# Nine step times in the planner of a state-space and attention trunk

## The chip, the cores and the metric

The kernel runs on one core of a Trainium2 chip. The metric is device microseconds (us) of one execution. Engines are called by their short names: PE is TensorE (matrix products; PEld is its weight load), DVE is VectorE, ACT is ScalarE, POOL is GpSimd, SP is the engine whose queue issues nearly all DMAs.

## The reference, cut to what matters

One call computes a trunk of two layers for 1024 latent tokens and 256 context tokens of width 1024: a state-space mixer (layer 0), attention (layer 1) and a final norm. The change touches the first layer alone:

```
z, xbc, dt = split(h @ in_w)                    # 2048 z, 4096 xbc, 64 dt columns
xbc = silu(conv of 5 taps along the tokens (xbc))
xs, B, C = split(xbc)                           # 8 groups of 4 heads of 64; B and C of 128 per group
la  = cumsum over 128 tokens of dt * a          # forward and backward in time
states = B^T (exp(la_end - la) * dt * xs)       # per chunk of 128 tokens
prev   = running sum of the states, decayed by exp(la_end)
y  = (C B^T * exp(la_l - la_s) * dt, causal) xs + (C prev) * exp(la)
out = rmsnorm((y_forward + y_backward + d * xs) * silu(z)) @ out_w
```

All of it is float32. A product of two float32 matrices is made from three matmuls on the parts "high" and "low" of each operand (`mm3`, L168 to L170).

## The kernel before, in words

The first layer, but for its output projection, is a list of steps and not a program written in order; two more such lists follow it, for the output projection and for the second layer. Each step is made by `plan.op(engine, function, after, rank, us, takes, uses)`: the engine that runs it, the steps it must follow, a rank (lower is sooner) and `us`, the time that the planner believes it takes. `takes` and `uses` name buffers from rings of fixed size. `Plan.order()` then plays all the steps through once, before the kernel is built: at each moment every engine that is free starts, of its steps whose inputs are ended and whose buffers are free, the one of lowest rank. The order in which steps were started there is the order in which their instructions are emitted. On the chip each engine works through its own queue strictly in that order, and waits where an input isn't there. So the numbers `us` change no instruction; they change which instruction stands ahead of which.

The steps around the change, for one core and all 1280 tokens (ten chunks of 128, in blocks of 256, 512 and 512):

- **Projections** (`load`, `project`): 48 tiles of 128 columns, 32 for the convolution and 16 for z. A tile's weights come in two halves `wraw`; ACT copies the high part `whi` (L599), and POOL and DVE in turn make the low part `wlo` (L602). PE makes 24 triples `pj` (L168 to L170).
- **Convolution** (`conv_tile`): ACT evicts the products to `ub` (L636) and makes the first tap (L642), DVE adds four taps (L645), ACT applies silu (L650). A ring of six tiles `ch` holds the results.
- **Mixing** (`mix`), once for each of eight groups, after its four convolution tiles: PE transposes (`tc`, L690), DVE or ACT copies to `xst` (L697, L695) and ACT to `Bt` (L701). `state`: POOL scales `xw` (L713), PE makes `st` (L718, two per step, nine steps), POOL decays the last state into `tm` (L732), DVE adds both into `PV` (L736). `wmat`: SP brings `lab` (L750), POOL masks it (L754), ACT takes four exponentials into `W` (L760), DVE adds the two directions (L773) and multiplies by the product of B and C (L775, with PE's L770), PE makes `yd` (L795). `y_out`: SP brings `es` (L832), PE makes `yo` (L837), DVE weighs it into `es` (L841), POOL or DVE adds up (L854), SP stores `y_d` (L861).
- **Columns for later** (`mod_later`): DVE accumulates rows of a weight for the second layer into `macc` (L900, L902), adds a bias (L923) and makes a low part (L931).
- Before all that: PE sums the columns of the first modulation (L304), the inputs are normalised and transposed (L331 to L367), and the step sizes `dv` are projected (L439 to L442, L453).

The planner fills PE with projections of later tiles and of z wherever a step of the mixing isn't ready.

Of the kernel before, what the change touches and what calls it, by code (L numbers as in the profile page):

```python
# [39 lines left out]
URGENT, LATE, DT_RANK = 30., 40., 15.  # L40
# [105 lines left out]
def emit(tc, A, out):  # L146
    nc = tc.nc
    V, S, G, T, Q = nc.vector, nc.scalar, nc.gpsimd, nc.tensor, nc.sync
# [106 lines left out]
    for b in ub:  # L255
# [4 lines left out]
    plan = Plan({"piece": 20, "xt": 4, "raw": 4, "wraw": 2, "mraw": 2, "wparts": 4, "pj": 2, "ub": 2, "ch": NCH, "zs": 2, "tc": 2,  # L260
                 "st": 1, "yd": 1, "yo": 1, "xst": 1, "Bt": 1, "PV": 1, "xw": 3, "tm": 1, "lab": NLAB, "W0": 2, "W1": 2, "es": 3})
# [321 lines left out]
    te_op, u_op, la_op, e_op, dec_ops = decays(step_sizes())  # L583
# [3 lines left out]
    def load(src, after=(), rank=0., raws="wraw"):  # L587

        raw, parts, t = plan.hold(raws), plan.hold("wparts"), {}
        odd = plan.turn("wlo")  # L590

        def bring():
            t["w"] = WR.raw_tile()
            Q.dma_start(t["w"], src)

        def high():
            t["hi"] = BIG.tile([128, 512], FR, tag="whi", bufs=4, name="whi")
            t["lo"] = BIG.tile([128, 512], FR, tag="wlo", bufs=4, name="wlo")
            S.activation(t["hi"], t["w"], AF.Copy)  # L599

        def low():
            (G if odd else V).tensor_tensor(t["lo"], t["w"], t["hi"].bitcast(FT), op=OP.subtract)  # L602

        a = plan.op("SP", bring, after, rank - 40, takes=[raw])
        a = plan.op("ACT", high, [a], rank - 30, .627, takes=[parts], uses=[raw])
        a = plan.op(*(("POOL", low, [a], rank - 30, 1.44) if odd else ("DVE", low, [a], rank - 30, .80)),
                    uses=[raw, parts])
        return t, parts, a

# [19 lines left out]
    def conv_tile(ct, rank):  # L629

        u, out, t = plan.hold("ub"), plan.hold("ch"), {}
        i, evs = plan.count("ub"), []
        for lo, hi, pt, bank, mm in project(16 + ct, rank):
            def evict(lo=lo, hi=hi, pt=pt):
                o = 2 if lo == 0 else 4
                S.activation(ub[i % 2][:, lo + o:hi + o], pt["p"], AF.Copy)  # L636
            evs.append(plan.op("ACT", evict, [mm] + evs[:1], rank - 1e4, .585 if hi - lo > 256 else .375,
                               takes=[u] if lo == 0 else [], uses=[u, bank]))

        def first():  # L640
            t["a"] = CH.tile([128, CW], FT, tag="ch", name="acc")
            S.activation(t["a"], ub[i % 2][:, 0:CW], AF.Copy, scale=convw[:, ct, 0:1])  # L642

        def tap(k):
            V.scalar_tensor_tensor(t["a"], ub[i % 2][:, k:k + CW], convw[:, ct, k:k + 1], t["a"], op0=OP.mult, op1=OP.add)  # L645

        a = plan.op("ACT", first, evs + [rest[0]], rank - URGENT, 1.364, takes=[out], uses=[u])
        for k in range(1, 5):
            a = plan.op("DVE", lambda k=k: tap(k), [a], rank - URGENT, 1.70, uses=[u, out])
        a = plan.op("ACT", lambda: S.activation(t["a"], t["a"], AF.Silu, bias=convb[:, ct:ct + 1]), [a, rest[1]], rank - URGENT, 1.367,  # L650
                    uses=[out], table="silu")
        return t, out, a
# [12 lines left out]
    def mix(g, chs, rank):  # L665
# [6 lines left out]
        def op(eng, f, after, us, **kw):  # L672
            seq[0] += .01
            return plan.op(eng, f, after, rank + seq[0], us, **kw)

        s = {}
        hxst, hBt, hPV = plan.hold("xst"), plan.hold("Bt"), plan.hold("PV")
        ready, blocks = {}, {}
# [27 lines left out]
        def state(i):  # L706
            bank, t, mms = plan.hold("st"), {}, []
            for d, c in ((0, i), (1, BORD[i])):
                hw = plan.hold("xw")

                def scale(d=d, c=c):
                    t[d] = pool["now"].tile([128, 4, 64], FT, tag="xw", bufs=3, name="xw")
                    G.tensor_tensor(t[d], s["xst"][:, c], te_t[:, d, c, h4][:, :, None].to_broadcast([128, 4, 64]), op=OP.mult)  # L713

                def product(d=d, c=c):
                    if d == 0:
                        t["st"] = psum("st", [128, 2, 4, 64])
                    T.matmul(flat(t["st"][:, d]), s["Bt"][:, c, :], flat(t[d]), start=True, stop=True)  # L718

                a = op("POOL", scale, [ready[c][0], te_op], .80, takes=[hw], uses=[hxst])  # L720
                mms.append(op("PE", product, [a, ready[c][1]] + mms, .44, takes=[bank] if d == 0 else [], uses=[bank, hw, hBt]))
            if i == 0:
                def keep():
                    s["PV"] = pool["now"].tile([128, 9, 2, 4, 64], FT, tag="PV", name="PV")
                    S.activation(s["PV"][:, 0], t["st"], AF.Copy)
                pv[0] = op("ACT", keep, mms, .604, takes=[hPV], uses=[bank, hPV])
            else:
                ht = plan.hold("tm")

                def decay():  # L730
                    t["tm"] = pool["now"].tile([128, 2, 4, 64], FT, tag="tm", bufs=1, name="tm")
                    G.tensor_tensor(t["tm"], s["PV"][:, i - 1], dec_t[:, i, :, h4][:, :, :, None].to_broadcast([128, 2, 4, 64]),  # L732
                                    op=OP.mult)

                a = op("POOL", decay, [pv[0]] + dec_ops, 1.11, takes=[ht], uses=[hPV])
                pv[0] = op("DVE", lambda: V.tensor_tensor(s["PV"][:, i], t["tm"], t["st"], op=OP.add), [a] + mms, .68,  # L736
                           uses=[ht, hPV, bank])

        def wmat(c):

            t0, t, ws, bank = tok0(c), {}, [], plan.hold("tc")
            for d in range(2):
                hl, hw = plan.hold("lab"), plan.hold(f"W{d}")
                sgn = 1 - 2 * d

                def bring(d=d):
                    t["l", d] = pool["now"].tile([128, 4, 128], FT, tag="lab", bufs=NLAB, name="lab")
                    src = bass.AP(tensor=la_d.tensor, offset=la_d.offset + (c * 64 + d * 32 + g * 4) * 128,
                                  ap=[[0, 128], [1, 512]])
                    Q.dma_start(flat(t["l", d]), src)  # L750


                def close(d=d, sgn=sgn):
                    G.affine_select(t["l", d], t["l", d], [[0, 4], [sgn, 128]], OP.is_ge, NEVER, base=0,  # L754
                                    channel_multiplier=-sgn)

                def expo(h, d=d):
                    if h == 0:
                        t["w", d] = pool["now"].tile([128, 4, 128], FT, tag=f"W{d}", bufs=2, name="W")
                    S.activation(t["w", d][:, h], t["l", d][:, h], AF.Exp, bias=u_t[:, d, c, 4 * g + h:4 * g + h + 1])  # L760

                a = op("SP", bring, third + [la_op], .38, takes=[hl])
                a = op("POOL", close, [a], .88, uses=[hl])
                for h in range(4):
                    a = op("ACT", lambda h=h, f=expo: f(h), [a, u_op], .312, takes=[hw] if h == 0 else [], uses=[hl, hw], table="exp")
                ws.append((hw, a))
# [48 lines left out]
        def y_out(bi, q):  # L815
# [4 lines left out]
            for d in range(2):  # L820
# [25 lines left out]
                last = g == NG - 1 and bi == 2  # L846
                eng, E, us = ("DVE", V, .75) if last else ("POOL", G, 1.5)
                if bi == 0:
                    eng, E, us = "DVE", V, .30

                def add(d=d, E=E, lo=lo, hi=hi):

# [32 lines left out]
    done = [None]  # L885

    def mod_later(n, q, rank):
# [3 lines left out]
        for kt in (2 * q, 2 * q + 1):  # L891
            raw, t = plan.hold("mraw"), {}

            def bring(kt=kt, t=t):
                t["w"] = pool["now"].tile([128, 512], FT, tag="mraw", bufs=2, name="mraw")
                Q.dma_start(t["w"], A["mod_w"][i, kt * 128:(kt + 1) * 128, ch * 512:(ch + 1) * 512])

            def add(j, kt=kt, t=t):
                if kt == 0:
                    V.tensor_scalar(macc[j], t["w"], cc[:, kt, j:j + 1], None, op0=OP.mult)  # L900
                else:
                    V.scalar_tensor_tensor(macc[j], t["w"], cc[:, kt, j:j + 1], macc[j], op0=OP.mult, op1=OP.add)  # L902

            a = plan.op("SP", bring, third, rank - 20, takes=[raw])
            for j in both:
                done[0] = plan.op("DVE", lambda j=j, f=add: f(j), [a, done[0]], rank, .92, uses=[raw])
        if q < 3:
            return
        hr, t = plan.hold("mraw"), {}
# [7 lines left out]
        for j in both:  # L917
# [23 lines left out]
            def store(j=j, k=k):  # L941
                Q.dma_start(m_d[j:j + 1, n * 512:(n + 1) * 512], t["r"][k:k + 1])

            a = plan.op("DVE", plus, [b, done[0]], rank, .70, uses=[hr])
            a = plan.op("ACT", high, [a], rank, .627, takes=[hp])
            a = plan.op("DVE", low, [a], rank, .80, uses=[hp])
            last.append(a)
# [952 lines left out]
```

## Time and profile before

| what | value |
|---|---|
| median of 3 runs (lowest, highest) | 2009.88 us (2005.18, 2011.53) |
| the profiled execution's own time | 2010.66 us |
| its span, first to last instruction | 2008.9 us |
| the first plan (up to the first product of the output projection) | 0 to 1020 us of the span |
| busy share of the span | PE 97%, DVE 72%, ACT 56%, POOL 59% |
| mean granted TensorE clock | 0.994 |

The profile gives the busy time of each engine, and for idle time the instruction that ended it. Matmuls overlap in the pipeline, so a busy PE is one that has a matmul under way. A line such as "PE st L718 <- POOL xw L713: 4.8, 5, 2.5" reads: PE, at the instructions of line 718 that write `st`, sat idle for 4.8 us in total, 5 times, 2.5 us at the longest, until POOL's `xw` of line 713 had ended. A group's line gives busy us and the mean of one in ns, and behind the second bar the idle time just ahead of it.

### The profile page before, as it was taken

To read this page: it belongs to the slowest core of one execution; us is meant where nothing else is said; L and a number is where in the kernel's file an instruction comes from. 1 tells how busy PE (TensorE), PEld (TensorE's weight loads), DVE (VectorE), ACT (ScalarE), POOL (GpSimd) and SP (SyncE) were. 2 spreads that over 40 slices of the span, in tenths; PEclk is the share of its full clock that TensorE was granted. 3 is DMA by queue.
4 is the path that set the end of the run, shared out by engine and by line. 5 is a ranking of instruction groups with operands and counts; after the bars stand their busy time and mean duration, and the time that the engine had idled before them with its cause. 6 is when DMAs were issued, how large, how long until landed. Compare 5 with 4: busy or idle time off the path is not lost.

```text
span 2008.9 us, 30605 instructions
## 1 busy us (share of the span) xinstructions
PE 1949.9 (97%) x10728; PEld 1497.8 (75%) x10728; DVE 1437.8 (72%) x1737; ACT 1116.9 (56%) x2047; POOL 1189.4 (59%) x973
## 2 busy tenths in 40 slices
PE   8899999999999999999999999999999999999998
PEld 8778888888888788888878878877775444444476
DVE  1485897786959786866445788768575888888643
ACT  2446767676766677676734676534224444554521
POOL 1201776666846576856459787855265667776722
PEclk9999999999999999999999999999999999999999
DMA  6114463635372545445586686553232111111033
GB/s 244 64 32 124 132 189 115 182 100 168 112 195 91 157 125 165 141 142 158 150 278 212 212 252 196 167 153 99 74 110 90 34 41 43 43 48 32 6 105 105
DMA packets 162126, 255.50 MB, mean 127 GB/s; under 512 B 21466, under 2 KB 57178, under 8 KB 161972
## 3 DMA queue, kind: packets, MB, share of 16 engines
q1 hardware_dynamic: 160820, 251.71, 40.5%
q8 instruction: 84, 1.38, 0.3%
q10 hardware_dynamic: 1152, 1.84, 0.3%
q14 instruction: 70, 0.57, 0.1%
HBM read 210.78 MB, written 42.63 MB: 126 GB/s over the span
## 4 chain that ended last, share of the span: by engine, by line
PE 75%; DVE 9%; DMA 5%; POOL 4%; issue 3%; ACT 3%; SPq 1%; DVEq 0%; POOLq 0%; ACTq 0%
PE pj L168 8%; PE pj L169 8%; PE pj L170 8%; PE sc L1663 7%; PE ot L1679 7%; PE ob L168 7%; PE ob L170 6%; PE ob L169 6%; DVE acc L645 4%; PE yo L837 2%; PE sc L1462 2%; PE st L718 2%; DMA spare<-in_mod_w 2%; PE yd L795 2%; PE sc L168 2%
## 5 line engine op out<-in xcount | busy, mean ns | idle before, releaser
L168 PE MATMUL pj<-inh,whi 128*128 128x512 f32 (+1 forms) x1152 | 441.7, 383 | 3.9 <-DVE dv L453 3.2
L170 PE MATMUL pj<-inh,wlo 128*128 128x512 f32 (+1 forms) x1152 | 410.7, 357 | 0.0
L169 PE MATMUL pj<-inl,whi 128*128 128x512 f32 (+1 forms) x1152 | 409.9, 356 | 0.8 <-POOL inl L367 0.8
L168 PEld LDWEIGHTS pj<-inh,whi 128*128 128x128 f32 x1152 | 219.1, 190 | 32.1 <-DVE dv L453 3.6
L645 DVE SCALAR_TENSOR_TENSOR acc<-ub,convw,acc 128x1282 f32<-128x1282 f32 x128 | 230.9, 1804 | 16.3 <-ACT acc L642 13.2
L170 PEld LDWEIGHTS pj<-inh,wlo 128*128 128x128 f32 x1152 | 218.2, 189 | 32.0
L169 PEld LDWEIGHTS pj<-inl,whi 128*128 128x128 f32 x1152 | 219.4, 190 | 26.5 <-POOL inl L367 1.2
L760 ACT ACTIVATE W<-lab,u_t 128x128 f32<-128x128 f32 x640 | 202.6, 390 | 62.5 <-POOL lab L754 39.7
L754 POOL TENSOR_SCALAR_AFFINE_SELECT lab<-lab 128x512 f32<-128x512 f32 x160 | 144.8, 911 | 147.3 <-DMA lab<-la_d 141.0
L1644 POOL TENSOR_TENSOR acc<-acc,P 128x1024 f32<-128x1024 f32 x80 | 192.5, 2406 | 64.4 <-ACT P L1668 62.7
L1668 ACT ACTIVATE P<-sc 128x1024 f32<-128x1024 f32 x160 | 162.9, 1025 | 115.4 <-PE sc L1663 106.4
L1609 DVE TENSOR_REDUCE mx<-sc 128x2 f32<-128x1024 f32 (+1 forms) x140 | 167.3, 1213 | 38.3 <-PE sc L1462 37.4
L713 POOL TENSOR_TENSOR xw<-xst,te_t 128x256 f32<-128x256 f32 x144 | 143.1, 1011 | 41.5 <-PE st L718 17.8
L1679 PE MATMUL ot<-P,vv 128*64 128x512 f32 x640 | 154.8, 605 | 0.0
L602 POOL TENSOR_TENSOR wlo<-wraw,whi 128x512 fp32r<-128x512 f32 x48 | 71.7, 1493 | 126.0 <-ACT whi L599 125.8
L1663 PE MATMUL sc<-q,kh 64*128 64x512 f32 x640 | 135.9, 420 | 0.5
L170 PE MATMUL ob<-whi,yl 128*128 128x512 f32 x288 | 113.5, 394 | 1.8 <-DVE yl L1061 1.8
L168 PE MATMUL ob<-whi,yh 128*128 128x512 f32 x288 | 114.2, 397 | 0.0
L169 PE MATMUL ob<-wlo,yh 128*128 128x512 f32 x288 | 113.3, 393 | 0.0
L1663 PEld LDWEIGHTS sc<-q,kh 64*128 64x128 f32 x640 | 60.0, 184 | 69.7 <-DVE mx L1609 29.6
L902 DVE SCALAR_TENSOR_TENSOR macc<-mraw,cc,macc 128x512 f32<-128x512 f32 x98 | 102.4, 1069 | 9.9 <-DMA mraw<-in_mod_w 9.8
L732 POOL TENSOR_TENSOR tm<-PV,dec_t 128x512 f32<-128x512 f32 x64 | 92.9, 1452 | 18.3 <-DVE PV L736 17.0
(281 smaller groups left out, 4504.6 us busy)
## 6 DMA issues: line engine op xcount, KB each, us to landing
lab<-la_d SPq DMA_DIRECT2D x160, 256.0 KB
wraw<-in_w_in SPq DMA_DIRECT2D x96, 256.0 KB
workvv<-in_m_out_w SPq DMA_DIRECT2D x94, 256.0 KB
mraw<-in_mod_w SPq DMA_DIRECT2D x64, 256.0 KB
es<-e_d SPq DMA_DIRECT2D x128, 128.0 KB
wraw<-in_wqkv SPq DMA_DIRECT2D x48, 256.0 KB
spare<-in_mod_w SPq DMA_DIRECT2D x32, 256.0 KB
q_d<-qs SPq DMA_DIRECT2D x64, 128.0 KB
```

The costliest lines, as they stand in the source:

```text
L168: T.matmul(o, lh, rh, start=first, stop=False)
L169: T.matmul(o, lh, rl, start=False, stop=False)
L170: T.matmul(o, ll, rh, start=False, stop=last)
L645: V.scalar_tensor_tensor(t["a"], ub[i % 2][:, k:k + CW], convw[:, ct, k:k + 1], t["a"], op0=OP.mult, op1=OP.add)
L713: G.tensor_tensor(t[d], s["xst"][:, c], te_t[:, d, c, h4][:, :, None].to_broadcast([128, 4, 64]), op=OP.mult)
L754: G.affine_select(t["l", d], t["l", d], [[0, 4], [sgn, 128]], OP.is_ge, NEVER, base=0, channel_multiplier=-sgn)
L760: S.activation(t["w", d][:, h], t["l", d][:, h], AF.Exp, bias=u_t[:, d, c, 4 * g + h:4 * g + h + 1])
L1609: V.tensor_reduce(max_place(t["m"][0], i), o, AX.X, OP.max)
L1644: E.tensor_tensor(t[e], t["P", k0] if two else t[e], t["P", kt], op=OP.add)
L1663: T.matmul(o[:, h], (first_row[r] if n == 3 else (kh, kl, kh)[n][r, kv, k]), x[(0, 0, 1, 2)[n]][r], start=(n == 0), stop=(n == 3))
L1668: S.activation(t["P", kt], flat(t["s", kt]), AF.Exp)
L1679: T.matmul(t["o"][h * 64:(h + 1) * 64], vv[:, kt, kv], t["P", kt][:, h * 512:(h + 1) * 512], start=(kt == 0), stop=(kt == NT - 1))
```

## The change

Nine arguments `us` in the first layer's plan get other values. No instruction, buffer, rank or dependency is edited.

```diff
 load, low part on DVE (L602)
-("DVE", low, [a], rank - 30, .80)
+("DVE", low, [a], rank - 30, 1.0)
 conv_tile, taps (L645)
-plan.op("DVE", lambda k=k: tap(k), [a], rank - URGENT, 1.70, ...
+plan.op("DVE", lambda k=k: tap(k), [a], rank - URGENT, 1.8, ...
 state, xw (L713)
-op("POOL", scale, [ready[c][0], te_op], .80, ...
+op("POOL", scale, [ready[c][0], te_op], 1.07, ...
 state, tm (L732)
-op("POOL", decay, [pv[0]] + dec_ops, 1.11, ...
+op("POOL", decay, [pv[0]] + dec_ops, 1.5, ...
 wmat, lab (L754)
-op("POOL", close, [a], .88, uses=[hl])
+op("POOL", close, [a], 1.0, uses=[hl])
 y_out, the adds of the first block on DVE (L854)
-eng, E, us = "DVE", V, .30
+eng, E, us = "DVE", V, .40
 mod_later, rows (L900, L902)
-plan.op("DVE", lambda j=j, f=add: f(j), [a, done[0]], rank, .92, ...
+plan.op("DVE", lambda j=j, f=add: f(j), [a, done[0]], rank, 1.05, ...
 mod_later, bias (L923)
-plan.op("DVE", plus, [b, done[0]], rank, .70, uses=[hr])
+plan.op("DVE", plus, [b, done[0]], rank, 1.1, uses=[hr])
```

The diff has eight edited lines for nine kinds of step, since L900 and L902 share one entry. From the first transposes of layer 0 up to its last step the order differs on all five engines; the two plans of the output projection and the second layer are untouched. The order's places that the prediction speaks of are shown there.

More of the change, by code (lines that the diff above doesn't have):

```diff
@@ L605, in load @@
         a = plan.op("ACT", high, [a], rank - 30, .627, takes=[parts], uses=[raw])
-        a = plan.op(*(("POOL", low, [a], rank - 30, 1.44) if odd else ("DVE", low, [a], rank - 30, .80)),
+        a = plan.op(*(("POOL", low, [a], rank - 30, 1.44) if odd else ("DVE", low, [a], rank - 30, 1.0)),
                     uses=[raw, parts])
@@ L648, in conv_tile @@
         for k in range(1, 5):
-            a = plan.op("DVE", lambda k=k: tap(k), [a], rank - URGENT, 1.70, uses=[u, out])
+            a = plan.op("DVE", lambda k=k: tap(k), [a], rank - URGENT, 1.8, uses=[u, out])
         a = plan.op("ACT", lambda: S.activation(t["a"], t["a"], AF.Silu, bias=convb[:, ct:ct + 1]), [a, rest[1]], rank - URGENT, 1.367,
@@ L718, in product @@
                     T.matmul(flat(t["st"][:, d]), s["Bt"][:, c, :], flat(t[d]), start=True, stop=True)
-                a = op("POOL", scale, [ready[c][0], te_op], .80, takes=[hw], uses=[hxst])
+                a = op("POOL", scale, [ready[c][0], te_op], 1.07, takes=[hw], uses=[hxst])
                 mms.append(op("PE", product, [a, ready[c][1]] + mms, .44, takes=[bank] if d == 0 else [], uses=[bank, hw, hBt]))
@@ L733, in decay @@
                                     op=OP.mult)
-                a = op("POOL", decay, [pv[0]] + dec_ops, 1.11, takes=[ht], uses=[hPV])
+                a = op("POOL", decay, [pv[0]] + dec_ops, 1.5, takes=[ht], uses=[hPV])
                 pv[0] = op("DVE", lambda: V.tensor_tensor(s["PV"][:, i], t["tm"], t["st"], op=OP.add), [a] + mms, .68,
@@ L762, in wmat @@
                 a = op("SP", bring, third + [la_op], .38, takes=[hl])
-                a = op("POOL", close, [a], .88, uses=[hl])
+                a = op("POOL", close, [a], 1.0, uses=[hl])
                 for h in range(4):
@@ L905, in mod_later @@
             for j in both:
-                done[0] = plan.op("DVE", lambda j=j, f=add: f(j), [a, done[0]], rank, .92, uses=[raw])
+                done[0] = plan.op("DVE", lambda j=j, f=add: f(j), [a, done[0]], rank, 1.05, uses=[raw])
         if q < 3:
@@ L942, in store @@
                 Q.dma_start(m_d[j:j + 1, n * 512:(n + 1) * 512], t["r"][k:k + 1])
-            a = plan.op("DVE", plus, [b, done[0]], rank, .70, uses=[hr])
+            a = plan.op("DVE", plus, [b, done[0]], rank, 1.1, uses=[hr])
             a = plan.op("ACT", high, [a], rank, .627, takes=[hp])
```

## The prediction

> **What bounds the kernel now.** First the page's head, then the busy time by stretches.
>
> ```profile
> span 2008.9 us, 30605 instructions
> PE 1949.9 (97%) x10728; PEld 1497.8 (75%) x10728; DVE 1437.8 (72%) x1737; ACT 1116.9 (56%) x2047; POOL 1189.4 (59%) x973
> ```
>
> ```profile
> core 0: us, PE busy (x) PEld busy (x) DVE busy (x) ACT busy (x) POOL busy (x), PEclk, DMA share, GB/s
> 112.00:1018.00 906.00, 890.66 (x5329) 759.55 (x5329) 683.63 (x789) 618.17 (x1233) 537.47 (x479) 1.00 0.48 141
> 0.00:112.00 112.00, 91.43 (x464) 84.59 (x465) 41.86 (x68) 44.51 (x74) 21.89 (x37) 1.00 0.40 142
> ```
>
> PE bounds the kernel. From 112 to 1018 us, where projections, convolution and mixing run, it lacks only 906.00 - 890.66 = 15.3 us; in the first 112 us it lacks 20.6. No step time changes PE's work, so an order can give back idle PE time only. The waits say what PE waited for in the long stretch (us in total, times, longest):
>
> ```profile
> PE tc L770 <- DVE W L775: 4.9, 6, 1.2
> PE st L718 <- POOL xw L713: 4.8, 5, 2.5
> PE yo L837 <- DVE es L841: 2.6, 5, 1.1
> PE st L718 <- DVE PV L736: 1.6, 3, 1.1
> PE tc L690 <- DVE xst L697: 0.7, 2, 0.4
> PE tc L690 <- ACT mr L939: 0.3, 1, 0.3
> ```
>
> Together 14.9 us in 22 short waits, all at places where PE leaves the projections for a step of the mixing: the plan had placed that step too early for the engine that feeds it. This sum caps the gain in the long stretch. In the first 112 us two waits are long:
>
> ```profile
> PE st L304 <- DMA spare<-in_mod_w: 13.4, 3, 8.5
> PE pj L168 <- DVE dv L453: 3.2, 1, 3.2
> ```
>
> ```profile
> 108.00:112.00 4.00, 1.12 (x8) 1.12 (x9) 3.42 (x4) 3.59 (x4) 0.27 (x1) 0.95 0.37 105
> 112.00:116.00 4.00, 4.00 (x23) 3.66 (x23) 1.67 (x4) 0.00 (x0) 0.00 (x0) 0.50 0.09 32
> 116.00:120.00 4.00, 4.00 (x17) 3.44 (x16) 0.81 (x2) 2.41 (x3) 0.00 (x0) 0.69 0.19 66
> ```
>
> The first is a load of weights ahead of every step that the change prices, and stays. The second is followed by a granted clock (the third number from the end) of 0.50 and 0.69: 4 x 0.50 + 4 x 0.31 + 4 x 0.05 = 3.4 us more are lost, so that wait of 3.2 costs 6.6 in all.
>
> **The change: how far the table was off.** For each edited step the groups give the busy us and the count (L602 is DVE's share of the low parts; L854 the adds of the first block):
>
> ```profile
> L713 POOL TENSOR_TENSOR xw<-xst,te_t 128x256 f32<-128x256 f32 x144 | 143.1, 1011 | 41.5 <-PE st L718 17.8 <-DVE xst L697 13.4 <-ACT xst L695 10.0
> L732 POOL TENSOR_TENSOR tm<-PV,dec_t 128x512 f32<-128x512 f32 x64 | 92.9, 1452 | 18.3 <-DVE PV L736 17.0 <-ACT PV L725 1.1
> L754 POOL TENSOR_SCALAR_AFFINE_SELECT lab<-lab 128x512 f32<-128x512 f32 x160 | 144.8, 911 | 147.3 <-DMA lab<-la_d 141.0 <-ACT W L760 2.5 <-DMA y_d<-es 1.9
> L645 DVE SCALAR_TENSOR_TENSOR acc<-ub,convw,acc 128x1282 f32<-128x1282 f32 x128 | 230.9, 1804 | 16.3 <-ACT acc L642 13.2
> L902 DVE SCALAR_TENSOR_TENSOR macc<-mraw,cc,macc 128x512 f32<-128x512 f32 x98 | 102.4, 1069 | 9.9 <-DMA mraw<-in_mod_w 9.8
> L900 DVE TENSOR_SCALAR macc<-mraw,cc 128x512 f32<-128x512 f32 x14 | 9.7, 725 | 3.5 <-DMA mraw<-in_mod_w 3.5
> L602 DVE TENSOR_TENSOR wlo<-wraw,whi 128x512 fp32r<-128x512 f32 x48 | 42.5, 885 | 16.0 <-ACT whi L599 16.0
> L923 DVE TENSOR_TENSOR macc<-macc,mr 1x512 f32<-1x512 f32 x14 | 16.2, 1181 | 0.0
> L854 DVE TENSOR_TENSOR es<-es,acc 128x128 f32<-128x128 f32 x32 | 10.2, 320 | 1.1
> ```
>
> POOL's three took 143.1 + 92.9 + 144.8 = 380.8 us. The old entries gave 144 x .80 + 64 x 1.11 + 160 x .88 = 327.0, short by 53.8; the new ones give 154.1 + 96.0 + 160.0 = 410.1, over by 29.3. DVE's steps took 411.9; old 128 x 1.70 + 112 x .92 + 48 x .80 + 14 x .70 + 32 x .30 = 378.4, short by 33.5; new 230.4 + 117.6 + 48.0 + 15.4 + 12.8 = 424.2, over by 12.3. The error falls from 87.3 to 41.6 us, to 0.48 of itself, and turns its sign: a feeder believed too slow puts PE's step later, behind one more projection, which costs PE nothing.
>
> So 14.9 x 0.52 = 7.7 us of the waits should go. But a table holds one number and the steps don't:
>
> ```profile
> L713 POOL TENSOR_TENSOR xw<-xst,te_t x144: 607/1020/1889, 202.3 to 961.1; 128x256 f32<-128x256 f32 x144
> L732 POOL TENSOR_TENSOR tm<-PV,dec_t x64: 1035/1478/2302, 207.8 to 966.6; 128x512 f32<-128x512 f32 x64
> ```
>
> Least, median and greatest ns: an `xw` near 1.9 us is late under 1.07 too. I take two thirds of the 7.7: a gain of 5.1 us, bounded by 14.9 (every wait goes) and 0 (as many new ones come).
>
> [...]
>
> **What moves, at two places.** POOL as the mixing begins: `lab` are masks, `wlo` the low half of a projection's weights; + and - are the change's rows and before's.
>
> ```order
>  L510 AFFINE_SELECT triu<-ones 128x128
>  L511 AFFINE_SELECT tril<-ones 128x128
>  L602 TENSOR_TENSOR wlo<-wraw,whi 128x512 x5
> -L754 AFFINE_SELECT lab<-lab 128x512
> -L602 TENSOR_TENSOR wlo<-wraw,whi 128x512
> +L754 AFFINE_SELECT lab<-lab 128x512 x3
> +L602 TENSOR_TENSOR wlo<-wraw,whi 128x512
> ```
>
> Three masks, each behind a DMA, now stand ahead of a low part that PE needs; one stood there before. In the trace of before (start, us):
>
> ```profile
> 183.87 0.64 POOL L754 TENSOR_SCALAR_AFFINE_SELECT lab<-lab 128x512 f32<-128x512 f32 x1 [10.34 <-DMA lab<-la_d]
> 185.61 1.29 POOL L602 TENSOR_TENSOR wlo<-wraw,whi 128x512 fp32r<-128x512 f32 x1 [1.11 <-ACT whi L599]
> 186.86 1.22 POOL L754 TENSOR_SCALAR_AFFINE_SELECT lab<-lab 128x512 f32<-128x512 f32 x2
> ...
> 187.83 0.28 PE L170 MATMUL pj<-inh,wlo 128*128 128x256 f32 x1
> ```
>
> The low part ended at 186.90, 0.9 us ahead of PE's first use of it. Two masks more are 1.2 us: if their loads have landed, `wlo` ends at 183.87 + 0.64 + 1.22 + 1.29 = 187.02 and nothing is lost; if the third landed only at 186.86, at 186.86 + 0.61 + 1.29 = 188.8, 0.9 late. On SP the write of `la_d`, from which the masks are loaded, now also stands behind a store of z that followed it:
>
> ```profile
> 167.87 0.62 SPq L579 DMA_DIRECT2D la_d<-laT  x1
> 169.21 1.28 SPq L663 DMA_DIRECT2D z_d<-zs  x1
> ```
>
> That is up to 169.21 - 167.87 = 1.3 us more. Bounds 0 and 2.2; I take a cost of 0.7, nearer to nothing, since the third load was issued together with the first.
>
> POOL at the start of the fourth group, where PE's longest wait of the stretch fell. Before:
>
> ```order
> L854 TENSOR_TENSOR es<-es,acc 128x512
> L754 AFFINE_SELECT lab<-lab 128x512
> L854 TENSOR_TENSOR es<-es 128x512
> L602 TENSOR_TENSOR wlo<-wraw,whi 128x512
> L713 TENSOR_TENSOR xw<-xst,te_t 128x256 x5
> L754 AFFINE_SELECT lab<-lab 128x512
> L732 TENSOR_TENSOR tm<-PV,dec_t 128x512
> ```
>
> and with the change:
>
> ```order
> L754 AFFINE_SELECT lab<-lab 128x512
> L602 TENSOR_TENSOR wlo<-wraw,whi 128x512
> L713 TENSOR_TENSOR xw<-xst,te_t 128x256
> L854 TENSOR_TENSOR es<-es,acc 128x512
> L713 TENSOR_TENSOR xw<-xst,te_t 128x256 x2
> L854 TENSOR_TENSOR es<-es 128x512
> L713 TENSOR_TENSOR xw<-xst,te_t 128x256 x2
> L754 AFFINE_SELECT lab<-lab 128x512
> L854 TENSOR_TENSOR es<-es,acc 128x512
> L732 TENSOR_TENSOR tm<-PV,dec_t 128x512
> ```
>
> The group's first `xw` no longer stand behind all adds `es` of the group before, but between them. In the order five groups of eight start so, one did before. The trace shows what stood ahead of the first `xw`:
>
> ```profile
> 492.06 2.52 POOL L854 TENSOR_TENSOR es<-es 128x512 f32<-128x512 f32 x1
> 494.54 2.52 POOL L602 TENSOR_TENSOR wlo<-wraw,whi 128x512 fp32r<-128x512 f32 x1
> 497.02 1.86 POOL L713 TENSOR_TENSOR xw<-xst,te_t 128x256 f32<-128x256 f32 x1
> ...
> 498.94 0.70 PE L718 MATMUL st<-xw,Bt 128*128 128x256 f32 x2 [2.50 <-POOL xw L713]
> ```
>
> That wait, 2.50 us, is a sixth of the 14.9, and should shorten; it is in the 5.1. Elsewhere I cost nothing: on DVE the rows from the four taps to the `dv` that PE waited for near 110 us are the same as before, so those 6.6 us stay (bounds: 0, or all 6.6 back), and behind the last `yo` the same projections follow, so the handover to the output projection is covered as before (bounds -1 and +1).
>
> Sum: -5.1 + 0.7 = -4.4 us on the profiled execution's 2010.66 us (span 2008.9 and 1.8 around it): **2006.3 us**. The profiled execution is 0.8 above the median of three.
>
> **Rivals.** (1) *As many waits come as go*: durations follow the neighbour engine and not the table. For it: the spread above. Against it: the old table was short on both engines, a bias and not a spread. 2010.7, give or take 3.
>
> (2) *Slower: the scalings `xw` get stuck between the adds.* Each add waits for DVE's `es`, POOL holds everything behind it, and PE's `st` stands soon after. The longest such wait, of 28:
>
> ```profile
> POOL es L854 <- DVE es L841: 44.1, 28, 5.2
> ```
>
> It decides from the point at which PE's wait reaches the 3.2 us of the `dv` wait, since then the clock halves as well: 6.6 us each. At two of the four new starts that is 13.2, 2006.3 + 13.2 = 2019.5; at one of them, 2012.9. Against it: the one group that starts so in before, near 270 us, shows nothing of it. PE's waits from 255 to 300 us are these two:
>
> ```profile
> PE tc L690 <- DVE xst L697: 0.3, 1, 0.3
> PE yo L837 <- DVE es L841: 0.2, 1, 0.2
> ```
>
> [...]
>
> (3) *The `dv` wait shrinks too.* The first transposes and parts are reordered ahead of it; if it falls under what halves the clock, 3.4 us come back, with the whole wait 6.6: 2006.3 - 3.4 = 2002.9 to 1999.7. Against it: the same rows on DVE.
>
> **How the numbers follow.** My forecast has 0.50, the first rival 0.17, the second 0.20, the third 0.13. About 0.3% (6.0 us) is what a measurement here can tell from no change. Within the forecast the gain runs from 0.5 to 12 us, and is over 6 in somewhat under half of the cases: 0.23 faster, 0.27 same. Rival 1 gives 0.02 faster, 0.14 same, 0.01 slower; rival 2 is slower, rival 3 faster. Faster 0.23 + 0.02 + 0.13 = 0.38; same 0.27 + 0.14 = 0.41; slower 0.01 + 0.20 = 0.21. The range runs from 1998, the forecast's 12 us with a little of rival 3, to 2018, rival 2 without its worse half.
>
> **What would show it.** Right: PE's waits from 112 to 1018 us near 9 us, `st <- POOL xw` and `tc <- DVE W` each about halved; PE idle at the first `st` of the fourth group under 2 us; the clock 0.50 behind the `dv` wait as before. Wrong: PE idle in this stretch of 15 us or more, a wait of over 3 us at a group's start with a granted clock under 1.00 behind it, or a first 112 us that differ by more than 2 us.

## The result, and the profile after

| | before | after |
|---|---|---|
| median of 6 runs (lowest, highest) | 2010.08 us (2005.18, 2011.53) | 1997.81 us (1994.03, 1998.78) |
| after / before | | 0.994, 95% interval 0.9929 to 0.995 |
| the profiled execution's own time | 2010.66 us | 1995.11 us |

The change makes the kernel 12.3 us faster. The profiled execution of after is 2.7 us under its median, so the 15.5 us between the two traces hold up to 3.3 us that belong to the execution and not to the change.

First the page's head of after, then its busy time by stretches. After's long stretch is cut at 1004 us, since its output projection begins some 14 us sooner. Its columns are those of the prediction's table: us, the busy time of PE, PEld, DVE, ACT and POOL, the granted clock, DMA share and GB/s.

```profile
span 1993.4 us, 30615 instructions
PE 1944.4 (98%) x10728; PEld 1497.3 (75%) x10728; DVE 1449.6 (73%) x1737; ACT 1111.8 (56%) x2042; POOL 1201.1 (60%) x973
```

```profile
0.00:112.00 112.00, 93.88 (x479) 87.21 (x480) 40.49 (x69) 44.27 (x74) 22.34 (x37) 0.99 0.40 143
112.00:1004.00 892.00, 884.57 (x5312) 759.04 (x5313) 693.36 (x788) 613.16 (x1228) 547.26 (x479) 1.00 0.48 143
```

PE makes the same 10728 matmuls. In the long stretch it lacks 892.00 - 884.57 = 7.4 us, where it lacked 15.3. What is left of its waits there:

```profile
PE tc L770 <- DVE W L775: 2.1, 4, 0.9
PE pj L168 <- ACT ub L636: 1.5, 1, 1.5
PE st L718 <- DVE PV L736: 1.1, 2, 0.9
PE st L718 <- ACT PV L725: 0.9, 1, 0.9
PE yo L837 <- DVE es L841: 0.6, 1, 0.6
PE st L718 <- POOL xw L713: 0.6, 1, 0.6
```

Ten waits of 6.8 us in all; before, 22 of 14.9. The wait for `xw` has nearly gone (4.8 to 0.6), that for `W` is under half (4.9 to 2.1), that for `es` a quarter (2.6 to 0.6).

To split the 15.5 us I compare three places in the two traces. PE goes on behind the `dv` wait at 110.88 us before and at 108.87 after: 2.0 us. The output projection's first product (L168, `tr`) starts at 1020.23 and at 1006.37: 13.9 us, of which 11.9 lie in the long stretch. The rest, to the end of the span, takes 988.7 and 987.0 us: 1.6 us. That last part is no work of the change. Ten us of it, from 20 us behind its start, before and then after (us, PE busy, granted clock, DMA share, GB/s):

```profile
1040.00:1050.00 10.00, 10.00 (x37) 0.83 0.92 317
```

```profile
1026.00:1036.00 10.00, 9.10 (x36) 1.00 0.90 322
```

The granted clock fell to 0.83 there in one execution and stayed at 1.00 in the other: 10 x 0.17 = 1.7 us.

**More came back than PE's waits show.** The waits in the long stretch fell by 14.9 - 6.8 = 8.1 us and the stretch by 11.9. The rows of matmuls overlap, and that hides a part of each stall (each place where PE's next matmul came late). Before, ahead of the fourth group's first `st`:

```profile
495.81 0.40 PE L169 MATMUL pj<-inl,whi 128*128 128x512 f32 x1
496.04 0.40 PE L170 MATMUL pj<-inh,wlo 128*128 128x512 f32 x1
```

Matmuls start 0.23 us apart and each has a row of 0.40. The next could have started at 496.27; it started at 498.94, so 2.67 us were lost. The wait's row said 2.50, since it counts from the end of the row before. By these rows a stall costs 0.40 - 0.23 = 0.17 us more than its row, and one of under 0.17 has no row. I take this for every stall, which is an estimate. The rows of the weight loads don't overlap there (0.19 us each, the same 0.23 apart); their waits with a releaser show how many stalls there were. Before, the long ones of 112 to 1004 us:

```profile
PEld tc L770 <- DVE W L775: 8.9, 12, 1.6
PEld st L718 <- POOL xw L713: 7.0, 6, 2.9
PEld yo L837 <- DVE es L841: 5.3, 7, 1.5
PEld st L718 <- DVE PV L736: 3.7, 6, 1.4
```

and after:

```profile
PEld tc L770 <- DVE W L775: 4.5, 8, 1.4
PEld yo L837 <- DVE es L841: 1.5, 3, 0.8
PEld st L718 <- DVE PV L736: 1.1, 1, 1.1
PEld st L718 <- POOL xw L713: 1.0, 1, 1.0
```

With the smaller groups these are 39 stalls before and 16 after, 18 with two that have a row of PE and no releaser here. (Their us, 28.1 and 10.4, are too much the other way: a weight load is issued ahead of its matmul, as at 182.39 us before, where its matmul starts at 182.61.) Of these, 22 had a row of PE before and 10 after. So 12 stalls with a row went, worth 12 x 0.17 = 2.0 more than their rows, and 17 - 8 = 9 without one, worth up to 9 x 0.17 = 1.5: 8.1 + 2.0 = 10.1 at least, 11.6 at most, beside the 11.9 measured; at least 0.3 us stay unexplained.

### The profile page after: what moved, and what is told of

It is laid out like the page before. It is cut to its first block, busy times and chain, and to the rows that moved or that the text cites. A ratio compares the mean times of both kernels' runs of the same rounds, so it can differ in the third digit from the quotient of the medians.

```text
span 1993.4 us, 30615 instructions
## 1 busy us (share of the span) xinstructions
PE 1944.4 (98%) x10728; PEld 1497.3 (75%) x10728; DVE 1449.6 (73%) x1737; ACT 1111.8 (56%) x2042; POOL 1201.1 (60%) x973
## 4 chain that ended last, share of the span: by engine, by line
PE 83%; DVE 7%; DMA 3%; ACT 2%; issue 2%; POOL 2%; SPq 1%; DVEq 0%; POOLq 0%; ACTq 0%
PE pj L168 10%; PE pj L170 9%; PE pj L169 9%; PE sc L1663 7%; PE ot L1679 7%; PE ob L168 7%; PE ob L170 6%; PE ob L169 6%; PE yo L837 3%; PE st L718 3%; DVE acc L645 2%; PE sc L1462 2%; PE yd L795 2%; DMA spare<-in_mod_w 2%; PE sc L170 1%
## 5 line engine op out<-in xcount | busy, mean ns | idle before, releaser
L168 PE MATMUL pj<-inh,whi 128*128 128x512 f32 (+1 forms) x1152 | 442.2, 384 | 4.9 <-DVE dv L453 3.4
L168 PEld LDWEIGHTS pj<-inh,whi 128*128 128x128 f32 x1152 | 219.1, 190 | 33.7 <-DVE dv L453 3.8
L645 DVE SCALAR_TENSOR_TENSOR acc<-ub,convw,acc 128x1282 f32<-128x1282 f32 x128 | 228.7, 1787 | 8.7 <-ACT acc L642 5.8
L713 POOL TENSOR_TENSOR xw<-xst,te_t 128x256 f32<-128x256 f32 x144 | 148.1, 1042 | 28.3 <-PE st L718 17.6
L602 POOL TENSOR_TENSOR wlo<-wraw,whi 128x512 fp32r<-128x512 f32 x48 | 72.1, 1501 | 123.0 <-ACT whi L599 119.9
L773 DVE TENSOR_TENSOR W<-W 128x512 f32<-128x512 f32 x80 | 80.0, 1000 | 47.9 <-ACT W L760 43.0
L168 PE MATMUL ob<-whi,yh 128*128 128x512 f32 x288 | 113.9, 395 | 0.0
```

The source lines that it names most:

```text
L168: T.matmul(o, lh, rh, start=first, stop=False)
```

## The experiments

**Theory.** The old table was short on both engines by a bias. The plan believed POOL and DVE sooner done than they were, and put PE's steps where their inputs weren't there. Tables nearer to the measured means move PE's steps to where their inputs are. **Rivals.** (R1) Luck of the order: any small edit of the table draws another order, and the times scatter; the change drew a good one. (R2) Slack: larger numbers are better as such, since a step of PE that comes late costs nothing; the change gains because it overshoots. (R3) One engine's entries do it all.

The entries are named `low` (L602), `tap` (L645), `xw`, `tm`, `lab`, `es` (L854 on DVE), `add` (L900, L902) and `bias` (L923); the table of before is called old, that of the change new. The runs were made in three sets, with runs of before in each (their medians 2009.43, 2011.05 and 2010.01 us); the ratios are to those. The waits are PE's from 112 to 1004 us in each kernel's profiled execution, in e7 to 1003, where its output projection begins.

| label | table | median us | to before, 95% interval | PE's waits, us |
|---|---|---|---|---|
| before | old | 2010.08 | | 14.9 |
| e4_old_nudged | old, each 1% up or down | 2013.83 | 1.0022 (1.0011 to 1.0033) | 17.5 |
| e5_old_nudged_back | the same, signs turned | 2021.70 | 1.0056 (1.0035 to 1.0078) | 19.0 |
| after | new | 1997.81 | 0.994 (0.9929 to 0.995) | 6.8 |
| e6_new_nudged | new, each 1% up or down | 1998.22 | 0.9937 (0.9921 to 0.9953) | 8.1 |
| e7_new_nudged_back | the same, signs turned | 1995.78 | 0.9926 (0.9908 to 0.9944) | 5.4 |
| e1_pool_only | new `xw`, `tm`, `lab`, else old | 2008.72 | 0.9991 (0.9982 to 1.0001) | 10.9 |
| e2_dve_only | the others new | 2004.01 | 0.9972 (0.9958 to 0.9986) | 14.2 |
| e3_exact_means | means of the trace of before | 1999.62 | 0.9945 (0.9931 to 0.996) | 7.8 |
| e9_short_twice | short by 2.5 times the old error | 2024.21 | 1.0068 (1.005 to 1.0085) | 28.1 |
| e10_over | new + (new - old) | 2039.10 | 1.0149 (1.0131 to 1.0166) | 26.4 |
| e8_dv_first | new, and `dv` ahead of the taps | 1994.65 | 0.9921 (0.9902 to 0.994) | 6.6 |
| e11_four_more | new, and four entries more | 1997.25 | 0.9939 (0.9924 to 0.9954) | 7.6 |
| e12_four_more_dv_first | both of these | 1992.41 | 0.9914 (0.9899 to 0.9929) | 6.8 |

### Is it the luck of the order? (e4 to e7)

Entries go up and down by 1% in turn: the error of the table hardly changes, the order is drawn anew. Three of the entries in e4 and e6:

```diff
-"DVE", low, .80      "POOL", scale, .80     "POOL", decay, 1.11
+"DVE", low, .792     "POOL", scale, .792    "POOL", decay, 1.121
-"DVE", low, 1.0      "POOL", scale, 1.07    "POOL", decay, 1.5
+"DVE", low, .990     "POOL", scale, 1.059   "POOL", decay, 1.515
```

> The old table with its entries moved by 1 per cent, up and down in turn (0.792, 1.717, 0.792, 1.121, 0.871, 0.303, 0.911, 0.707): the order differs but the error is the same. Theory: 2010 give or take 3, PE's waits as before. Rival (luck of the order): more than 5 us away from the kernel before is as likely as not.

> The old table moved by 1 per cent the other way round (0.808, 1.683, 0.808, 1.099, 0.889, 0.297, 0.929, 0.693). Theory: the error is as large as in the old table, so 2010 give or take 4, as the first nudge gave 2014. Rival (luck of the order): as likely under 2004 as not.

> The change's table with its entries moved by 1 per cent, up and down in turn (0.99, 1.818, 1.059, 1.515, 0.99, 0.404, 1.04, 1.111). Theory: the error stays small, so 1998 give or take 4. Rival (luck of the order): the change's own order was the lucky one, and this one falls back to 2004 to 2012.

> The change's table moved by 1 per cent the other way round (1.01, 1.782, 1.081, 1.485, 1.01, 0.396, 1.061, 1.089). Theory: 1998 give or take 4. Rival (luck of the order): 2004 to 2012.

Three orders from the old table took 2010, 2014 and 2022 us, three from the new one 1998, 1998 and 1996. The order does scatter, and far more under the old table than I had expected (e5 is 11.7 us above the 2010 expected, where 4 was allowed). But the worst of the new ones is 12 us better than the best of the old. The traces say the same: the output projection's first product starts at 1020.2, 1026.7 and 1028.0 us under the old table, at 1006.4, 1010.5 and 1003.1 under the new one. R1 falls. In e5 the largest group of waits is again the one for `W`:

```profile
PE tc L770 <- DVE W L775: 7.0, 8, 3.4
```

The same feeder as in before, with a single wait of 3.4 us where the longest was 1.2.

A part of the scatter is the clock. Among waits of 2.9 us (e4) and of 2.9 and 3.4 us (e5) the granted clock is 0.50 for 6.8 us from 231.1 us in e4, and for 6.8 us from 229.9 and again from 240.1 us in e5. PE is busy for 5.5 and 11.3 us of these, so up to 2.8 and 5.6 us are lost. In before, after, e6 and e7 the clock is 1.00 from 120 us to the output projection.

### Which engine's entries? (e1, e2)

Half of the table each; what e1 takes from the change and e2 leaves out:

```diff
-"POOL", scale, .80   "POOL", decay, 1.11    "POOL", close, .88
+"POOL", scale, 1.07  "POOL", decay, 1.5     "POOL", close, 1.0
```

> The three POOL entries new (xw 1.07, tm 1.5, lab 1.0), the DVE entries as before. Theory (the old table was short, so PE met its feeders too soon): POOL held 53.8 of the 87.3 us of error, so rather more than half of the 12 us gained: 2003 us, 7 under the kernel before, with PE's waits for xw nearly gone and those for W left. Rival (any shift of the table draws another order, and this change drew a lucky one): no relation to the size of the error, anything from 1996 to 2014.

> The DVE entries new (low part, taps, adds of the first block, rows, bias), the three POOL entries as before. Theory: 33.5 of the 87.3 us of error, so 4 to 5 us under the kernel before, 2005 us; PE's waits for W and es fall, those for xw stay at some 5 us. Rival (luck of the order): anything from 1996 to 2014.

e1 missed: it is 0.7 us faster, which can't be told from nothing. Its waits:

```profile
PE tc L770 <- DVE W L775: 4.4, 8, 1.0
PE yo L837 <- DVE es L841: 3.4, 5, 1.1
...
PE pj L168 <- ACT ub L636: 0.8, 1, 0.8
PE tc L690 <- ACT Bt L701: 0.7, 1, 0.7
PE st L718 <- POOL xw L713: 0.3, 1, 0.3
```

POOL's own wait went as it should, 4.8 to 0.3. Those for DVE's `W` and `es` stayed, and PE then met ACT's `ub` and `Bt`, and at the handover waited 1.72 us for ACT's `whi`: a part of the waits moved on to ACT, whose times were not edited. The wait for `whi` is not e1's alone, though: e6 and e7 have it too, with 1.2 us each.

e2's time came out as expected, its waits did not: that for `W` fell (4.9 to 3.9), that for `es` did not (2.6 to 2.9), that for `xw` is 2.8 us where some 5 were expected, and one of 3.5 us for ACT's `ub` is new. Its trace is of an execution of 2008.51 us, where the median is 2004.01, so its waits say little about the median.

Beside before's 2009.43 us in the same set the halves gain 0.7 and 5.4, together 6.1; the whole change gains 12.3. Neither engine's entries did it all here, so R3 is not borne out. That both feeders have to be right, since a step of PE waits for the latest of its inputs, would explain why the halves don't add up. But each half is a single order, and orders of the old table scatter by up to 12 us, so this stays argued.

### Accuracy, or more slack? (e3, e9, e10)

e3 takes the means of the trace of before (`bias` 1.18 as measured, `tm` 1.452 and so on); e9 and e10 take the change's step once more, downwards from old and upwards from new. By the prediction's counts e9 is short of the trace by 216 us and e10 over it by 170, where old was short by 87.3 and the change over by 41.6:

```diff
 low   tap    xw     tm     lab   es    add   bias
-1.0   1.8    1.07   1.5    1.0   .40   1.05  1.1     (new)
+.885  1.804  1.011  1.452  .911  .32   1.03  1.18    (e3)
+.60   1.60   .53    .72    .76   .20   .79   .30     (e9)
+1.20  1.90   1.34   1.89   1.12  .50   1.18  1.50    (e10)
```

> All nine steps get the mean that the trace of before shows (xw 1.011, tm 1.452, lab 0.911, taps 1.804, low part 0.885, rows 1.03, bias 1.18, adds 0.32). Theory: the bias is gone, so as fast as the change, 1998 give or take 3. If it is the overshoot of the change's entries that helps (a feeder believed slower than it is, PE's step later), it stays 3 to 6 slower, 2001 to 2004. Rival (luck of the order): anything from 1996 to 2014.

> The old table moved by the size of the change in the other direction (low part 0.60, taps 1.60, xw 0.53, tm 0.72, lab 0.76, adds 0.20, rows 0.79, bias 0.30): the table is about twice as short against the trace. Theory (steps believed too fast put PE's steps too early): slower by another 10 us or more, 2020 to 2030, PE's waits for xw, PV and W over 20 us. Rival (luck of the order): about 2010 to 2020.

> The change made twice over (low part 1.20, taps 1.90, xw 1.34, tm 1.89, lab 1.12, adds 0.50, rows 1.18, bias 1.50): the table is now too long against the trace by more than it was too short. If a feeder believed too slow costs PE nothing, as the prediction had it, 1996 to 2001. If an error costs the same both ways, back to 2005 to 2012.

e3 does all but 1.8 us of what the change does, without its overshoot. e9 is 14 us slower than before. Two of its three largest groups of waits grew, those for `W` (4.9 to 8.9) and `PV` (1.6 to 7.1); that for `xw` stayed at 4.8.

```profile
PE tc L770 <- DVE W L775: 8.9, 9, 2.5
PE st L718 <- DVE PV L736: 7.1, 7, 2.3
PE st L718 <- POOL xw L713: 4.8, 6, 1.2
```

All of its waits are 28.1 us, or 25.6 without the `dv` wait, which here falls behind 112 us. By time alone e9 does not stand clear of the old table's own scatter, since e5 took 2021.70; by the start of the output projection it does (1036.7 us, e5 1028.0).

e10 is the surprise. If a feeder believed too slow cost nothing, it would have stayed near 1998; it is 29 us slower than before, the slowest of all. R2 falls, and with it a sentence of the prediction. First its largest group of waits in the long stretch:

```profile
PE tc L770 <- DVE W L775: 17.0, 9, 4.7
```

That is two thirds of its 26.4 us, for steps whose own times (.75 in the plan for L773, .68 for L775) were not raised. The longest of them, and what stood ahead of it on ACT and DVE:

```profile
357.53 1.28 ACT L660 ACT_TABLE_LOAD   x1
358.82 0.60 ACT L660 ACTIVATE zs<-pj 128x512 f32<-128x512 f32 x1
359.43 1.28 ACT L760 ACT_TABLE_LOAD   x1
360.73 2.45 ACT L760 ACTIVATE W<-lab,u_t 128x128 f32<-128x128 f32 x8
...
363.21 0.69 DVE L773 TENSOR_TENSOR W<-W 128x512 f32<-128x512 f32 x1 [2.08 <-ACT W L760]
...
364.68 0.80 PE L770 MATMUL tc<-acc 128*128 128x128 f32 x2 [4.72 <-DVE W L775]
```

ACT made a silu of z between exponentials, with a table load before and behind it (1.28 + 0.60 + 1.28 = 3.2 us), so DVE's sum came late and PE behind it. So PE was again sent to a step whose input was late, now by way of steps whose times had not been raised. That the unraised times are the reason is argued; no run raised every entry alike.

Second, too few projections were left for the end of the mixing. The last stretch of the plan in e10, and the last row ahead of the output projection's first product:

```profile
990.00:1020.00 30.00, 23.63 (x144) 19.29 (x141) 14.21 (x25) 18.26 (x42) 12.71 (x15) 0.83 0.48 121
1020.00:1050.00 30.00, 21.87 (x130) 19.02 (x128) 9.32 (x14) 5.00 (x9) 6.66 (x9) 0.93 0.60 195
```

```profile
1041.24 0.40 PE L170 MATMUL pj<-inh,wlo 128*128 128x512 f32 x1
1049.76 0.77 PE L168 MATMUL tr<-whi,yh 128*128 128x512 f32 x1 [8.13 <-DVE yh L1058]
```

PE idled 6.4 and 8.1 us in these two stretches, at a clock of 0.83 and 0.93; the first is waits for `W`, `xw` and `es` (3.7, 2.0, 0.6), the second is one wait at the handover. The last `yo` ran at 1039.88, and three matmuls of a projection were left behind it, 1.0 us. In after the last `yo` runs at 995.23 and 10 us of projections follow. Each step put later uses up projections ahead of it, and these are finite; I take that for the price of believing a feeder too slow, but one order is all there is of it.

Third, the clock. The first product of the output projection comes 29.5 us later than before. The waits account for 11.5 of these and the handover for 8.1. The rest fits the clock: it is 0.50 for 20.3 us from 243.8, 6.8 from 363.2, 6.7 from 581.7 and 10.1 from 994.7, with PE busy for 33.0 us of them, so up to 16.5 us are lost, where before lost 3.4 behind the `dv` wait.

### The wait near 110 us (e8)

Here `dv`, for which PE waits 3.4 us in after, is ranked ahead of the convolution's taps on DVE:

```diff
-            done.append(step("DVE", both, [a], .68 if w5 else .41, uses=[bank]))
+            done.append(plan.op("DVE", both, [a] + second, -100 + b, .68 if w5 else .41, uses=[bank]))
```

> The change's table, and the three additions that end the step sizes get a rank ahead of the convolution's taps, so that DVE takes them between the taps. Theory: the wait of PE near 109 us (3.4) and the half clock behind it (3.4) go, 5 to 7 us under the change, 1992. If the later order moves with it and waits come back there, 1996 to 2002.

Its median is 3.2 us under the change's, between the two expectations, and less than medians here tell apart; the trace shows where it can come from, as the first plan's order on PE and DVE differs from after's at the `dv` steps and the matmuls around them alone. The wait is 1.9 us, as two taps (4.06 us) still stand ahead on DVE. The clock behind it was to stay up, and did so only in part. PE busy, granted clock, DMA share and GB/s in after and then in e8:

```profile
104.00:108.00 4.00, 1.48 (x7) 1.00 0.12 39
108.00:112.00 4.00, 3.13 (x23) 0.80 0.32 98
112.00:116.00 4.00, 4.00 (x16) 0.50 0.18 66
116.00:120.00 4.00, 4.00 (x16) 0.84 0.00 0
```

```profile
108.00:112.00 4.00, 2.83 (x17) 0.90 0.41 135
112.00:116.00 4.00, 4.00 (x20) 0.67 0.22 68
116.00:120.00 4.00, 4.00 (x19) 1.00 0.00 0
```

After loses 4 x (0.20 + 0.50 + 0.16) = 3.4 us to the clock there, e8 4 x (0.10 + 0.33) = 1.7. So 1.5 us of the wait and 1.7 of the clock came back, 3.2 together. At the output projection's first product 2.7 of them are left (1003.63 us, after 1006.37). The two traces as a whole differ by only 0.7 us, since what follows took 989.1 us in e8 and 987.0 in after.

### What the table still leaves (e11, e12)

Four more entries go towards the means of the trace of after (1.00, 1.50, 1.07 and 1.67 us); that of L931 goes to its mean in before instead:

```diff
-L773 "DVE" .75    L602 "POOL" 1.44    L931 "DVE" .80    L854 "POOL" 1.5
+L773 "DVE" .95    L602 "POOL" 1.5     L931 "DVE" .85    L854 "POOL" 1.67
```

> The change's table, and four steps that it left take the means of the trace of the change: the sum of the two directions W 0.75 to 0.95, POOL's low part 1.44 to 1.5, the low part of the later columns 0.80 to 0.85, POOL's adds 1.5 to 1.67. Theory: PE's waits for W (2.1) and es (0.6) shrink, 1 to 4 us under the change, 1995. Rival (the change has already found what is to be found): 1998 give or take 3.

> The four further steps and the additions of the step sizes ahead of the taps, both on the change's table. Theory: both gains add, 1992 give or take 3. If the four further steps do nothing, 1995 as with the additions alone.

e11 equals the change within the measurement. Neither wait shrank: that for `W` is 2.6 us (2.1 in after), that for `es` 2.8 (0.6). Behind one of 2.6 and one of 1.9 us the clock is 0.50 for 3.4 us each time, and at the handover PE waits 1.75 us for ACT's `whi`. So what is left of PE's waits is not mended by these four entries. e12 at 1992.41 us is the fastest of all, below both kernels, but most of it is the `dv` edit's: over e8 it has 2.2 us, less than the 6 that can be told apart here.

## Why the prediction was right and wrong

**The mechanism was right, the size was not.** Faster by 12.3 us, where 4.4 was forecast; 1997.81 is 0.2 us under the range's low end. By the traces the long stretch gave 11.9 us where I took 5.1, the start 2.0 where I took nothing, and the masks cost nothing where I took 0.7; 1.6 more is the clock of one execution. The step that failed is the first term, in two places. Of the 6.8 us it lacked, 2.6 are the shade of two thirds, 0.4 the factor 0.52, and 3.8 lie outside PE's rows. For these the fault is in the sentence "This sum caps the gain in the long stretch": 14.9 us of PE's idle rows. They leave out what the pipeline covers. With 0.17 us for each of the 22 stalls and up to 0.17 for each of the 17 without a row, the stalls of before cost 14.9 + 3.7 + up to 2.9, so 18.6 to 21.5 us. The gain did not pass the 14.9, but as a cap they were too low. The prediction's own factor, 0.52, on 18.6 to 21.5 gives 9.7 to 11.2; the stretch gave 11.9.

**The shade of two thirds was not needed.** I cut the 7.7 us to 5.1 because a table holds one number and the steps vary threefold. By the rows that the estimate was made from, 8.1 us went. The spread is still there: after the change an `xw` takes 604 to 1976 ns, where it took 607 to 1889, and 18 of 39 stalls are left. For the order the mean is what to mend, as e3 shows.

**"Which costs PE nothing" was wrong**, as e10 shows, though at the change's own overshoot (29.3 and 12.3 us of some 400 each) nothing is seen to be lost to it: e3 without the overshoot is no faster.

**The masks ahead of `wlo` cost nothing**, where I took 0.7. After, on POOL:

```profile
181.46 0.64 POOL L754 TENSOR_SCALAR_AFFINE_SELECT lab<-lab 128x512 f32<-128x512 f32 x1 [9.59 <-DMA lab<-la_d]
...
184.38 0.63 POOL L754 TENSOR_SCALAR_AFFINE_SELECT lab<-lab 128x512 f32<-128x512 f32 x1 [0.61 <-DMA es<-e_d]
184.98 1.29 POOL L602 TENSOR_TENSOR wlo<-wraw,whi 128x512 fp32r<-128x512 f32 x1
```

The first mask came 2.4 us sooner than before (183.87), as did the program by 2.0, and the low part ended at 186.27; no wait for it is among PE's. The lower bound was right.

**The start.** The `dv` wait stayed (3.2 before, 3.4 after) with a clock of 0.50 behind it, as forecast. But the first 112 us were to differ by no more than 2 us, and PE got past that wait 2.01 us sooner, so that sign of being wrong was met, if barely. Of these, 0.35 us were there already at 58 us (58.49 before, 58.14 after), behind the load that the change doesn't touch. The first transposes wait less (`tc` for `raw` 2.3 before; `inl` and `inh` 0.8 and 0.7 before, gone after):

```profile
PE st L304 <- DMA spare<-in_mod_w: 12.9, 2, 8.6
PE pj L168 <- DVE dv L453: 3.4, 1, 3.4
PE tc L354 <- DVE raw L361: 1.4, 2, 1.2
PE tc L354 <- ACT raw L359: 0.3, 1, 0.3
```

That is the place which the third rival named and whose small part I had costed at nothing: 2.3 - 1.4 - 0.3 + 1.5 = 2.1 us by the rows.

**The fourth group.** The wait of 2.50 us is gone altogether; the one wait for `xw` left is of 0.57 us, in the fifth group.

**The rivals.** The first, that as many waits come as go, fell: stalls fell from 39 to 18. Its premise has something in it: in the trace of before an `xw` with no instruction of DVE beside it took 0.61 us (the mean of 8), one beside DVE for over nine tenths of its time 1.11 (the mean of 111 of the 144). What makes it longer, no run shows, and the mean was enough for the table all the same. The part of this rival that held is the scatter of the old table's orders (e4, e5). The second, `xw` stuck between the adds at a group's start, has no wait of PE at any of the five starts; its condition was never met. It and the third took the 3.2 us of the `dv` wait for the point from which the clock halves. That, with the 6.6 us for each such wait, was one row of before, and no run shows such a point: behind a wait of 3.4 us the clock stayed at 1.00 in e7, behind one of 1.9 us it was 0.50 for 3.4 us in e8. The slower side was real, with long waits and the clock at 0.50 behind them, but in larger errors of either sign (e9, e10) and in two orders of the old table (e4, e5).

## What to carry to other kernels

A planner's step times should be the means measured beside the other engines (an `xw`: 0.61 us with DVE idle, 1.01 in the mean of all), on every engine that feeds the one that bounds. Here mending one engine's times gained 0.7 or 5.4 us of 12.3, and overstating the times by 170 us in all cost 29. Count stalls by the weight loads' waits and add to each idle row of PE what the pipeline hides (here 0.17 us), before calling their sum a cap. Look at the granted clock behind each longer wait, since half clock can cost as much as the wait (in before 3.4 us behind one of 3.2). And before a table's edit is credited or blamed, nudge its entries by 1% both ways: here that alone moved the time by up to 12 us on the old table, and by 2 on the new one.

## What was not expected of the hardware

**The clock falls for whole pieces of 3.4 us, and an idle time of 3.4 us doesn't always lower it.** In e7 PE waited 3.4 us for `dv`, as in after, and the granted clock stayed at 1.00 up to the output projection:

```profile
104.00:108.00 4.00, 0.94 (x5) 1.00 0.18 67
108.00:112.00 4.00, 3.64 (x32) 1.00 0.25 70
112.00:116.00 4.00, 4.00 (x21) 1.00 0.20 66
```

In e8 a wait of 1.9 us did lower it. The clock's records in the traces are 1.00 or 0.50, and a slice's mean is made of these two. So the time at half clock behind the `dv` wait is twice what was lost: before 2 x 3.4 = 6.9 us (0.05, 0.50 and 0.31 of 4 us each), after 6.9 (0.20, 0.50, 0.16), e8 3.4 (0.10, 0.33), e7 none. These are two, two, one and no pieces of 3.4 us. In e6 it is three, behind the same wait of 3.4 us (0.54, 0.50 and 0.68 in the three slices), and in e10 one, behind 3.2. By its records before is at 0.50 for 6.827 us from 111.63, 3.413 from 1040.06 and 6.827 from 1907.04 us, after for 6.827 from 110.43 and 3.413 from 1892.18. The last record of each, from 2002.62 and 1987.76 us, has no matmul under it, runs on behind the last instruction and is no whole number of pieces (8.344 and 7.654 us). In each of the two traces all falls start on one grid: in before 272, 526 and 554 pieces of 3.4133 us behind the first, in after 522 and 550.

How long PE waited does not decide by itself whether the clock falls, nor for how long: a wait of 3.4 us was followed by 6.8 us at 0.50 in after, by three pieces in e6 and by none in e7, one of 1.9 us by one piece in e8. What else decides, no run here shows.

After's own runs spread from 1994 to 1999 us: its two fastest had a mean clock of 0.996, the others 0.994 or 0.995. That the spread comes from this alone is argued.
